# Token halves of the output projection swapped, the norm's gain moved into the FFN weights, and four rings re-used

## The chip, the cores and the metric

The kernel runs on one core of one Trainium2 chip. The metric is the device time of one execution in microseconds (us). Engine names: PE is TensorE's matmul, ACT is ScalarE, DVE is VectorE, POOL is GpSimd, SP is SyncE, which here issues every DMA transfer.

## What is computed

A trunk of two layers over 1024 tokens of width 1024, in float32. Layer 0 mixes by attention, layer 1 by a gated recurrence; each is followed by a gated feed-forward network (FFN) of inner width 2816. Every sub-layer has a norm ahead of it and one behind it.

```python
def rmsnorm(x, g):
    y = x * rsqrt(mean(x * x, axis=-1) + 1e-6)
    return y * g

for layer in range(2):
    h = rmsnorm(x, norm_mix_pre[layer])
    m = attention(h) @ attn_w_out  if layer == 0 else  recurrence(h) @ rg_w_out
    x = x + rmsnorm(m, norm_mix_post[layer])
    h = rmsnorm(x, norm_ffn_pre[layer])
    f = (silu(h @ w_gate) * (h @ w_up)) @ w_down
    x = x + rmsnorm(f, norm_ffn_post[layer])
```

## The kernel before

**Products.** Float32 accuracy comes from three fast matmuls: each operand is split into a rounded high part (an ACT cast) and the rest, the low part (a DVE subtraction), and PE adds high x high, high x low, low x high. A product of 128 x 512 outputs over a depth of 512 is 12 such matmuls. The FFN's products are cut by a Strassen-Winograd scheme: seven products where a plain block product has eight, at the price of sums of blocks (S1 to S4 on the weights' side, the tiles e and f on the tokens' side).

**Tokens** are handled in tiles of 128: tiles 0 to 3 are the first half, 4 to 7 the second.

**out_product** is the projection behind each mixer with both norms. It takes six tiles in two trios, first (0,1,4), then (2,3,5), each trio in six PSUM banks, and last the tiles 6 and 7 as plain float32 matmuls from unsplit weights, 16 matmuls each; those weight rows lie in the ring "w" (eight buffers of 4 KB per partition). For each tile it runs `post_norm` (L209) and `pre_norm` (L187): DVE multiplies the PSUM result by the gain into the tile mg (L215), ACT squares and sums (L168), POOL makes the inverse root rs (L170 to L172), DVE adds to x (L218), then ACT squares x, POOL makes the next rs, DVE makes h = x * rs * g (L195), PE transposes h in eight 128 x 128 pieces (L201), and `HiddenS.take` (ACT L75, DVE L78) builds the tokens' operands from the transposes: b0 from a first-half tile (its transposes are also kept, in f), b1 and b2 from a second-half tile together with the f of its partner. mg is also the buffer of h.

**gate_up** multiplies by the gate and up weights, 11 column groups each. `begin` makes ahead of time the two products of a column group that need b0 alone, for the first two groups of each. `blocks` loads a group's two weight tiles of 128 x 1024, makes the sums, casts each operand (`operand`, ACT L493, DVE L494) and runs the products, S2's first. With the two begun ones a block is seven products of 12 matmuls. **down** makes seven products into the rows of a result r = 0 or 1 of four tiles a each. It finishes row 1 first, runs the norms `norm(1, a)`, then the last products, and for each a the norm `norm(0, a)`. Row r, tile a is token tile 4*r + a: the second half comes first. Behind layer 0's `down` the hidden tiles go to **recurrent** instead, whose `xr` runs, for three column groups c, 24 matmuls over the first token half (L158 to L160) and then 24 over the second.

The order of the instructions on each engine is set by the scheduler when the kernel is built, from its own estimate of times. Each engine then runs its list strictly in order and waits on semaphores; SP does the same with the DMA list. A ring's buffer is free for its next tile when the last reader of the old one is through.

Of the kernel before, what the change touches and what calls it, by code (L numbers as in the profile page):

```python
# [45 lines left out]
class HiddenS:  # L46
# [5 lines left out]

    GROUPS = ((0, 2), (2, 1), (3, 4))

    def __init__(self, trunk, pool):
        self.nc, self.uid = trunk.nc, trunk.uid
        self.g = [[pool.tile([P, n, 4, 512], F32R, tag=f"b{i}{z}", name=trunk.uid("hS"))
                   for z in range(2)] for i, (_, n) in enumerate(self.GROUPS)]
        self.f = {}
# [6 lines left out]
    def take(self, t, ps, scratch, pool):  # L66
# [25 lines left out]
        f, e = self.f[t - 4], new("e", 1)  # L92
# [10 lines left out]
class Trunk:  # L103
# [4 lines left out]
    def __init__(self, ctx, tc, io):  # L108
# [15 lines left out]
        self.mark = None  # L124

# [61 lines left out]
    def pre_norm(self, pool, x, h, g, sink, t, psum):  # L187
# [9 lines left out]
        for q in range(2):  # L197
            ps = psum()
            for j in range(4):
                kt = 4 * q + j  # L200
                nc.tensor.transpose(ps[:, j * P:(j + 1) * P], h[:, kt * P:(kt + 1) * P], self.ident)  # L201
# [3 lines left out]
    def post_norm(self, ms, mg, x_src, x_dst, t, gpost, sink, pool, g=None):  # L205
# [14 lines left out]
        if sink is not None:  # L220
            self.pre_norm(pool, x, mg, g, sink, t, self.psum_t)
# [188 lines left out]
    def out_product(self, ap, aT, w, x_src, x_dst, gpost_v, g_v, sink, kts):  # L410
# [24 lines left out]
        def norm(t, ps):  # L435
            mg = ap.tile([P, D], F32, tag="mg", bufs=2, name=self.uid("mg"))
            ms = [(slice(i * 512, (i + 1) * 512), p) for i, p in enumerate(ps)]
            self.post_norm(ms, mg, x_src, x_dst, t, gpost, sink, ap, g)

        gpost = g = None  # L440
        bufs = {"act": 2, "ah": 3, "al": 3}
        for ts in ((0, 1, 4), (2, 3, 5)):
            pst = [[self.psum() for _ in range(2)] for _ in range(3)]
            for kt in kts:
                if g is None and kt == kts[0]:
# [13 lines left out]
            if g is None:  # L459
                gpost = self.gain(ap, "gpost", gpost_v)  # L460
                g = self.gain(self.apool, "first", g_v)
            for i in ((0, 1, 2) if ts[0] == 0 else (0, 2, 1)):
                norm(ts[i], pst[i])

        rows, acts = [], []
        for i, kt in enumerate(kts):
            raw = self.main.tile([P, 2, 512], F32, tag="w", bufs=8, name=self.uid("raw"))
            nc.sync.dma_start(raw, wv[kt])
            rows.append(raw)
            n = ("ah", "al", "act")[i % 3]  # L470
            acts.append(act(kt, (6, 7), ap.tile([P, 384], F32, tag=n, bufs=bufs[n], name=self.uid("act"))[:, :2 * P]))
        for t in range(2):
# [3 lines left out]
            norm(6 + t, ps)  # L476


    def gate_up(self, ap, hS, wg, wu, gO):
# [5 lines left out]
        nc, tt = self.nc, self.nc.vector.tensor_tensor  # L485
        n_op = [0]

        def operand(src):

            pool, tag, bufs = (self.main, "w", 8) if n_op[0] % 14 < 8 else (ap, "w2", 6)  # L490
            n_op[0] += 1
            t = pool.tile([P, 2, 4, P], F32R, tag=tag, bufs=bufs, name=self.uid("q"))
            self.last = nc.scalar.copy(t[:, 0], src).ins  # L493
            tt(t[:, 1], src, t[:, 0].bitcast(F32), op=ALU.subtract)  # L494
            return t

        def raw():
            return self.main.tile([P, 2, 4, P], F32, tag="raw", bufs=3, name=self.uid("raw"))

        def rows(w, k, c0, n):  # L500
            return w[k * 512:(k + 1) * 512, c0:c0 + n].rearrange("(k p) c -> p k c", p=P)
# [10 lines left out]
        def begin(w, j):  # L512

            r = raw()
            for k in range(2):
                nc.sync.dma_start(r[:, k], rows(w, k, j * 256, P))
            a11, a12 = operand(r[:, 0]), operand(r[:, 1])
            return product(a11, 0), product(a12, 1)

        def sums(p1, p2):  # L520
            c = [ap.tile([P, 512], F32, tag="c", bufs=11, name=self.uid("c")) for _ in range(4)]
            nc.scalar.copy(c[1], p1)  # L522
            tt(c[0], p2, c[1], op=ALU.add)
            return c

        def blocks(w, j, begun=None, after=None):


            a = []
            for k in range(2):  # L530
                r = raw().rearrange("p z k c -> p (z k c)").rearrange("p (k c) -> p k c", k=4)
                nc.sync.dma_start(r, rows(w, k, j * 256, 256))
                a.append(r)
            a11, a21 = a[0][:, :, 0:P], a[0][:, :, P:256]
            a12, a22 = a[1][:, :, 0:P], a[1][:, :, P:256]
            with self.tc.issue_after(after) if after else nullcontext():
                if begun is None:
                    begun = [product(operand(a11), 0), None]
                    begun[1] = product(operand(a12), 1)
                q = {}  # L540
                q["A22"] = operand(a22)
                tt(a22, a21, a22, op=ALU.add)
                tt(a21, a11, a21, op=ALU.subtract)
                tt(a11, a22, a11, op=ALU.subtract)
                q["S2"] = operand(a11)
                q["S3"] = operand(a21)
                q["S1"] = operand(a22)
                tt(a12, a12, a11, op=ALU.subtract)
                q["S4"] = operand(a12)
# [411 lines left out]
```

## Time and profile before

| | |
|---|---|
| median of 3 runs | 2275.26 us (2273.81 to 2275.34) |
| the profiled execution | 2271.51 us, span 2269.7 us |
| busy share of the span: PE, DVE, ACT, POOL | 97%, 70%, 44%, 7% |
| mean granted TensorE clock | 0.99 |
| stages: o0 (out_product, layer 0), then its FFN | about 514 to 617 us, 617 to 1285 us |
| recurrent; o2 (out_product, layer 1); its FFN | 1285 to 1510 us, 1514 to 1615 us, 1615 us to the end |

A row of the timeline gives the start, the length, the engine, the source line, the operation, what it writes and reads, its shape, and in brackets the idle time of the engine ahead of it with the instruction that ended it. Matmuls overlap: a 128 x 512 one is shown 0.39 us long, but the next starts 0.23 us behind it. A row of the groups gives busy us in all and mean ns of one, then the idle time ahead of them.

### The profile page before, as it was taken

Reading aid. Unit: us, or ns where it says so; the run is one execution under the profiler, and the core shown is the slowest. Engines: PE = TensorE matmul, PEld = TensorE weight load, DVE = VectorE, ACT = ScalarE, POOL = GpSimd, SP = SyncE. Lnnn points to the kernel's source line nnn. Section 1 sums busy time; section 2 is a strip of 40 time slices with the busy share of each in tenths; the row PEclk is TensorE's granted clock in tenths of the full one; section 3 lists DMA queues with packets and bytes.
Section 4 is the critical chain, followed back from the end, with each engine's and each line's share of the span. In section 5 each row is a group of like instructions: output and inputs, shape, how many; then the busy total and the mean of one; then the engine's idle time right before and its main releaser. Section 6 shows DMA issues by size and latency. Waiting matters only on the chain. (4 is left out here: it accounts for less than half of the span.)

```text
span 2269.7 us, 29965 instructions
## 1 busy us (share of the span) xinstructions
PE 2201.2 (97%) x10968; PEld 1794.1 (79%) x10968; DVE 1592.3 (70%) x2476; ACT 999.9 (44%) x1738; POOL 163.8 (7%) x370
## 2 busy tenths in 40 slices
PE   7999999999999999999999799999899999999998
PEld 6887888877678888888888577887578888888886
DVE  5676765464678777775867577626788777758676
ACT  4544455464543333332536567525533333324444
POOL 2111212131100000000001100001100000000010
PEclk9999999999999999999999899999999999999999
DMA  4101011125724333234558311257434333327456
GB/s 161 55 19 48 24 43 40 59 94 162 248 70 139 116 92 118 89 121 171 191 166 263 120 47 47 83 169 245 134 112 134 93 116 93 116 89 275 122 193 235
DMA packets 200100, 278.84 MB, mean 123 GB/s; under 512 B 14224, under 2 KB 127888, under 8 KB 199952
## 3 DMA queue, kind: packets, MB, share of 16 engines
q1 hardware_dynamic: 199952, 276.92, 38.0%
q8 instruction: 86, 1.41, 0.3%
q14 instruction: 62, 0.51, 0.1%
HBM read 211.33 MB, written 65.54 MB: 122 GB/s over the span
## 5 line engine op out<-in xcount | busy, mean ns | idle before, releaser
L507 PE MATMUL ps<-hS,q 128*128 128x512 f32 x1232 | 482.6, 392 | 13.4 <-ACT c L522 10.1
L508 PE MATMUL ps<-hS,q 128*128 128x512 f32 x1232 | 481.7, 391 | 1.5 <-DVE hS L78 1.5
L509 PE MATMUL ps<-hS,q 128*128 128x512 f32 x1232 | 481.0, 391 | 0.0
L493 ACT CAST q<-raw 128x512 fp32r<-128x512 f32 x308 | 187.0, 621 | 410.5 <-PE ps L509 154.4
L507 PEld LDWEIGHTS ps<-hS,q 128*128 128x128 f32 x1232 | 232.4, 189 | 65.0 <-ACT c L522 11.2
L508 PEld LDWEIGHTS ps<-hS,q 128*128 128x128 f32 x1232 | 232.7, 189 | 50.4 <-DVE hS L78 2.3
L509 PEld LDWEIGHTS ps<-hS,q 128*128 128x128 f32 x1232 | 232.5, 189 | 48.6
L494 DVE TENSOR_TENSOR q<-raw,q 128x512 fp32r<-128x512 f32 x308 | 209.1, 689 | 67.4 <-ACT q L493 64.4
L605 PE MATMUL ps<-o,o 128*128 128x512 f32 x616 | 239.8, 390 | 0.6 <-DVE o L600 0.6
L606 PE MATMUL ps<-o,o 128*128 128x512 f32 x616 | 237.6, 390 | 0.0
L604 PE MATMUL ps<-o,o 128*128 128x512 f32 x616 | 220.1, 391 | 3.2 <-ACT o L715 2.5
L599 ACT CAST o<-raw 128x512 fp32r<-128x512 f32 x206 | 123.8, 620 | 188.7 <-PE ps L606 57.7
L600 DVE TENSOR_TENSOR o<-raw,o 128x512 fp32r<-128x512 f32 x206 | 137.9, 688 | 58.1 <-ACT o L599 57.1
L148 DVE TENSOR_TENSOR wlo<-raw,whi 128x1024 fp32r<-128x1024 f32 x76 | 93.3, 1229 | 75.6 <-ACT whi L147 73.4
L604 PEld LDWEIGHTS ps<-o,o 128*128 128x128 f32 x616 | 115.4, 188 | 29.7 <-ACT o L715 4.4
L605 PEld LDWEIGHTS ps<-o,o 128*128 128x128 f32 x616 | 115.6, 188 | 25.0 <-DVE o L600 1.3
L606 PEld LDWEIGHTS ps<-o,o 128*128 128x128 f32 x616 | 115.6, 188 | 24.2 <-DVE o L716 0.4
L171 POOL TENSOR_SCALAR rs<-ss 128x1 f32<-128x1 f32 x64 | 25.7, 401 | 1267.4 <-ACT junk L168 1174.4
L147 ACT CAST whi<-raw 128x1024 fp32r<-128x1024 f32 x76 | 79.8, 1052 | 70.2 <-PE ps L159 24.7
L158 PE MATMUL psq<-hT,whi 128*128 128x512 f32 x256 | 101.2, 395 | 1.1 <-DVE v L255 1.1
L159 PE MATMUL psq<-hT,whi 128*128 128x512 f32 x256 | 100.9, 394 | 0.0
L160 PE MATMUL psq<-hT,wlo 128*128 128x512 f32 x256 | 100.5, 393 | 0.0
(184 smaller groups left out, 4103.4 us busy)
## 6 DMA issues: line engine op xcount, KB each, us to landing
raw<-in_ffn_w_down_dram SPq DMA_DIRECT2D x96, 256.0 KB, 4.3
raw<-in_ffn_w_gate_dram SPq DMA_DIRECT2D x44, 512.0 KB, 4.2
raw<-in_ffn_w_up_dram SPq DMA_DIRECT2D x44, 512.0 KB, 4.0
gS<-c SPq DMA_DIRECT2D x88, 256.0 KB, 2.2
raw<-gS SPq DMA_DIRECT2D x88, 256.0 KB, 2.8
gA<-c SPq DMA_DIRECT2D x66, 256.0 KB, 3.2
raw<-in_attn_w_in_dram SPq DMA_DIRECT2D x24, 512.0 KB, 4.0
raw<-in_attn_w_out_dram SPq DMA_DIRECT2D x24, 512.0 KB, 4.2
```

The source lines that it names most:

```text
L158: nc.tensor.matmul(ps, wh[:, kt, cols], hh[:, kt, :], start=kt == 0, stop=False)
L159: nc.tensor.matmul(ps, wh[:, kt, cols], hl[:, kt, :], start=False, stop=False)
L493: self.last = nc.scalar.copy(t[:, 0], src).ins
L494: tt(t[:, 1], src, t[:, 0].bitcast(F32), op=ALU.subtract)
L507: nc.tensor.matmul(ps, a[:, 0, kt, :], bh, start=kt == 0, stop=False)
L508: nc.tensor.matmul(ps, a[:, 0, kt, :], bl, start=False, stop=False)
L509: nc.tensor.matmul(ps, a[:, 1, kt, :], bh, start=False, stop=kt == 3)
L599: nc.scalar.copy(t[:, 0], src)
L600: tt(t[:, 1], src, t[:, 0].bitcast(F32), op=ALU.subtract)
L604: nc.tensor.matmul(ps, a[0], b[:, 0], start=first, stop=False)
L605: nc.tensor.matmul(ps, a[0], b[:, 1], start=False, stop=False)
L606: nc.tensor.matmul(ps, a[1], b[:, 0], start=False, stop=last)
```

## The change

The token halves change places: out_product takes the trios (4,5,0) and (6,7,1) and then the plain tiles 2 and 3; `HiddenS` builds b0 from tiles 4 to 7 and b1, b2 from tiles 0 to 3; `down` maps row r, tile a to tile 4*(1-r) + a, so that the first token half is normed first and the second last. `pre_norm` of the FFN no longer multiplies by the gain: ACT makes h = x * rs, and the 512 KB load of that gain goes. The gain is applied to the weights instead: in `begin` by four ACT and four DVE instructions of 128 x 128 for an operand that was one of each of 128 x 512, and in `blocks` by eight ACT instructions of 128 x 256, in place, ahead of the sums. The first mg of each trio, the f of tile 7 and the first two pairs of begun results take buffers of the ring "w"; the weight rows of the plain tiles are loaded ahead of the second trio's norms, two of the eight rows in the ring "raw" (three buffers), where the FFN's weights are loaded too. The second and third begun pairs are ordered behind the transposes of tiles 2 and 3. Silu is called within `blocks`. The diff, cut:

```diff
-        if t < 4:
-            f = self.f[t] = new("f", 2)
+        if t >= 4:
+            f = self.f[t - 4] = new("f", 2) if t != 7 else self.spare()
...
-        def norm(t, ps):
-            mg = ap.tile([P, D], F32, tag="mg", bufs=2, name=self.uid("mg"))
+        def norm(t, ps, own=True):
+            mg = (ap.tile([P, D], F32, tag="mg", bufs=2, name=self.uid("mg")) if own else
+                  self.main.tile([P, D], F32, tag="w", bufs=8, name=self.uid("mg")))
...
-        for ts in ((0, 1, 4), (2, 3, 5)):
+        for ts in ((4, 5, 0), (6, 7, 1)):
...
-            for i in ((0, 1, 2) if ts[0] == 0 else (0, 2, 1)):
-                norm(ts[i], pst[i])
-
-        rows, acts = [], []
-        for i, kt in enumerate(kts):
-            raw = self.main.tile([P, 2, 512], F32, tag="w", bufs=8, name=self.uid("raw"))
+            else:
+                rows, acts = [], []
+                for i, kt in enumerate(kts):
+                    tag, n = ("raw", 3) if i < 2 else ("w", 8)
+                    raw = self.main.tile([P, 2, 512], F32, tag=tag, bufs=n, name=self.uid("raw"))
...
+            for i in range(3):
+                norm(ts[i], pst[i], i > 0)
...
+                src, k0 = src
+                for k in range(4):
+                    g = gain[:, k0 + k:k0 + k + 1]
+                    nc.scalar.activation(t[:, 0, k], src[:, k], AF.Copy, scale=g)
+                    nc.vector.scalar_tensor_tensor(t[:, 1, k], src[:, k], g, t[:, 0, k].bitcast(F32),
+                                                   op0=ALU.mult, op1=ALU.subtract)
...
+            a = [operand((raw(w, k, j * 256, P, r[:, k]), 4 * k), False) for k in range(2)]
+            with self.tc.issue_after(after) if after else nullcontext():
+                return product(a[0], 0), product(a[1], 1)
...
+                    for i in range(4):
+                        nc.scalar.activation(a[k][:, i], a[k][:, i], AF.Copy, scale=gain[:, 4 * k + i:4 * k + i + 1])
...
-            begun[i] = begin(w, j)
+            begun.append(begin((wg, wu)[i % 2], i // 2, self.turned[i + 1] if i in (1, 2) else None))
             if i < 2:
-                begun[i] = sums(*begun[i])
+                o = self.main.tile([P, 2, 512], F32, tag="w", bufs=8, name=self.uid("first"))
+                nc.scalar.copy(o[:, 0], begun[i][0])
+                tt(o[:, 1], begun[i][1], o[:, 0], op=ALU.add)
+                begun[i] = o
...
-                    self.post_norm(ms, mg, x_src, x_dst, 4 * r + a, gpost, sink, ap)
+                    self.post_norm(ms, mg, x_src, x_dst, 4 * (1 - r) + a, gpost, sink, ap)
```

How the scheduled order moves is seen at two places. **PE, end of layer 0's `down`, before.** `pst<-ident` are the transposes of the last normed tiles, m1722 and m1723 being the hidden tiles a = 2 and 3 of row 0; `ps<-hT` is `xr` on the first token half (hT1925 its high part), on the second (hT1927).

```order
L606 MATMUL ps2066_11648<-o2014_11387,o2065_11645 128x512
L201 MATMUL pst2058_11619<-ident_63,m1722_9722 128x128 x4
L201 MATMUL pst2059_11624<-ident_63,m1722_9722 128x128 x4
L201 MATMUL pst2073_11700<-ident_63,m1723_9723 128x128 x4
L201 MATMUL pst2074_11705<-ident_63,m1723_9723 128x128 x4
L158 MATMUL ps2092_11760<-hT1925_10973,whi2076_11734 128x512
```

**The same place in the change**, where m1723 and m1724 are the tiles a = 2 and 3 (token tiles 6 and 7), hT1926 and hT1927 the high and low part of the first half, and hT1928 the high part of the second:

```order
L163 MATMUL ps2096_12018<-hT1926_11197,wlo2081_11966 128x512
L204 MATMUL pst2059_11843<-ident_63,m1723_9946 128x128 x4
L161 MATMUL ps2096_12018<-hT1926_11197,whi2080_11965 128x512
L162 MATMUL ps2096_12018<-hT1927_11198,whi2080_11965 128x512
L204 MATMUL pst2060_11848<-ident_63,m1723_9946 128x128 x4
L163 MATMUL ps2096_12018<-hT1926_11197,wlo2081_11966 128x512
...
L163 MATMUL ps2099_12052<-hT1926_11197,wlo2084_11973 128x512
L204 MATMUL pst2074_11924<-ident_63,m1724_9947 128x128 x4
L204 MATMUL pst2075_11929<-ident_63,m1724_9947 128x128 x4
L161 MATMUL ps2102_12086<-hT1928_11199,whi2077_11958 128x512
```

All 72 matmuls of `xr` on the first token half, 24 for each of ps2093, ps2096 and ps2099, now stand between the transposes of the last normed tiles and in part ahead of them; before, they stood behind the last transpose.

**ACT, start of layer 0's `gate_up`, before.** hS is written by `take` for the last tile, whose e and f are e1275 and f1233 (L75), c is a begun result, q1306 the operand A22 of the first block and q1307 that of its S2.

```order
L75 CAST hS1058_5604<-f1211_6273 128x2x4x128
L75 COPY e1275_6507<-pst1273_6497 128x512
L75 CAST hS1056_5602<-pst1274_6502 128x4x128
L75 CAST hS1058_5604<-e1275_6507 128x8x128
L75 CAST hS1058_5604<-f1233_6356 128x2x4x128
L522 COPY c1282_6626<-ps1279_6599 128x512
L493 CAST q1306_6746<-raw1305_6744 128x512
L522 COPY c1291_6667<-ps1288_6640 128x512
L570 ACT_TABLE_LOAD
L570 ACTIVATE c1281_6625<-c1281_6625 128x512
L493 CAST q1307_6752<-raw1304_6742 128x512
```

**The same place in the change**, where q1294 is a begun operand, the raw tiles are weights scaled in place by the gain, e1274 and f1237 belong to the last tile, q1299 is the operand A22 and q1300 that of S2:

```order
L77 CAST hS1058_5604<-e1261_6443 128x8x128
L508 ACTIVATE q1294_6747<-raw1292_6735,gcol_72 128x128 x2
L77 CAST hS1056_5602<-pst1273_6500 128x4x128
L77 CAST hS1058_5604<-f1226_6303 128x2x4x128
L543 ACTIVATE raw1298_6784<-raw1298_6784,gcol_72 128x256 x3
L77 COPY e1274_6505<-pst1272_6495 128x512
L543 ACTIVATE raw1298_6784<-raw1298_6784,gcol_72 128x256
L77 CAST hS1058_5604<-e1274_6505 128x8x128
L77 CAST hS1058_5604<-f1237_6342 128x2x4x128
L543 ACTIVATE raw1313_6892<-raw1313_6892,gcol_72 128x256 x4
L502 CAST q1299_6794<-raw1298_6784 128x512
L502 CAST q1300_6800<-raw1297_6782 128x512
```

The casts for the last tile and S2's operand now stand behind scaling instructions of two weight tiles and of begun operands, while the table load (L570 before) and the copies of begun results have left this place.

More of the change, by code (lines that the diff above doesn't have):

```diff
@@ L510, in product @@
             return ps
-        def begin(w, j):
-            r = raw()
-            for k in range(2):
[L516 to L533, printed above, removed]
+        def begin(w, j, after):
+            r = self.main.tile([P, 2, 4, P], F32, tag="raw", bufs=3, name=self.uid("raw"))
+            a = [operand((raw(w, k, j * 256, P, r[:, k]), 4 * k), False) for k in range(2)]
+            with self.tc.issue_after(after) if after else nullcontext():
+                return product(a[0], 0), product(a[1], 1)
@@ L534, in blocks @@
+        def blocks(w, j, begun, silu, after=None):
+            a = [raw(w, k, j * 256, 256) for k in range(2)]
+            for k in range(2):
+                with self.tc.issue_after(after) if after else nullcontext():
+                    for i in range(4):
+                        nc.scalar.activation(a[k][:, i], a[k][:, i], AF.Copy, scale=gain[:, 4 * k + i:4 * k + i + 1])
             a11, a21 = a[0][:, :, 0:P], a[0][:, :, P:256]
             a12, a22 = a[1][:, :, 0:P], a[1][:, :, P:256]
[L536 to L549, printed above, removed]
@@ L550, in blocks @@
-            c = sums(*begun) if len(begun) == 2 else begun
-            _, u2, u3, c22 = c
-            tt(u2, product(q["S2"], 4), u2, op=ALU.add)
+            q = {}
+            if begun is None:
+                q["A11"] = operand(a11)
+                q["A12"] = operand(a12)
+            q["A22"] = operand(a22)
+            tt(a22, a21, a22, op=ALU.add)
+            tt(a21, a11, a21, op=ALU.subtract)
+            tt(a11, a22, a11, op=ALU.subtract)
+            q["S2"] = operand(a11)
+            q["S3"] = operand(a21)
@@ new lines, in blocks @@
+            q["S1"] = operand(a22)
+            tt(a12, a12, a11, op=ALU.subtract)
+            q["S4"] = operand(a12)
+            c = [ap.tile([P, 512], F32, tag="c", bufs=11, name=self.uid("c")) for _ in range(4)]
+            c11, u2, u3, c22 = c
+            if begun is None:
+                begun = product(q["A11"], 0), product(q["A12"], 1)
+            if isinstance(begun, tuple):
+                nc.scalar.copy(u2, begun[0])
+                tt(c11, begun[1], u2, op=ALU.add)
+                p1, sum = u2, c11
+            else:
+                p1, sum = begun[:, 0], begun[:, 1]
@@ L553, in blocks @@
+            tt(u2, product(q["S2"], 4), p1, op=ALU.add)
             tt(u3, product(q["S3"], 5), u2, op=ALU.add)
@@ L913, in run @@
                                  io["rg_w_out"], xs[1], xs[2], io["norm_mix_post"][1],
[L914 removed]
+                                 hS, list(range(KT)))
             if stop == 2:
```

83 lines of the change are left out of this document (47 added, 36 removed).

## The prediction

> **What bounds the kernel now.** I read the page's busy shares first, then the table by stage, then PE's timeline where a stage is short of full.
>
> ```profile
> PE 2201.2 (97%) x10968; PEld 1794.1 (79%) x10968; DVE 1592.3 (70%) x2476; ACT 999.9 (44%) x1738; POOL 163.8 (7%) x370
> ```
>
> PE is busy 97% of the span: all its idle time is 2269.7 - 2201.2 = 68.5 us, and no change that leaves the products alone can win more than that and the time in which matmuls run slowly. Here the number of PE's instructions stays the same. The columns of the next table are the length, each engine's busy time (with its instructions), the granted clock, the DMA engines' share and GB/s.
>
> ```profile
> core 0: us, PE busy (x) PEld busy (x) DVE busy (x) ACT busy (x) POOL busy (x), PEclk, DMA share, GB/s
> 510.00:700.00 190.00, 179.66 (x765) 134.96 (x762) 129.77 (x177) 85.07 (x153) 15.10 (x40) 0.96 0.49 159
> 700.00:1200.00 500.00, 500.00 (x2206) 413.77 (x2205) 373.20 (x580) 177.02 (x300) 0.00 (x0) 1.00 0.42 135
> 1200.00:1300.00 100.00, 85.65 (x383) 68.31 (x382) 70.19 (x96) 61.53 (x103) 19.84 (x32) 0.91 0.61 195
> 1510.00:1700.00 190.00, 177.97 (x743) 135.22 (x743) 131.90 (x181) 87.92 (x156) 15.10 (x40) 0.98 0.54 176
> ```
>
> The long inner part of the FFN, 700 to 1200 us, has no PE idle time at all; a matmul there takes 500 / 2206 = 0.227 us. What can be won lies at the seams: 14.4 us idle at a clock of 0.91 in 1200 to 1300, where layer 0's `down` hands over to the recurrence, and 10 to 12 us each in 510 to 700 and 1510 to 1700, from out_product into `gate_up`. The change touches both kinds of seam, and puts work into the full part.
>
> **Seam one: `down` to the recurrence.** PE's timeline:
>
> ```profile
> 1261.62 1.10 PE L201 MATMUL pst<-ident,m 128*128 128x128 f32 x8 [0.32 <-ACT m L193]
> 1262.47 0.48 PE L606 MATMUL ps<-o,o 128*128 128x512 f32 x1
> ...
> 1268.75 1.09 PE L201 MATMUL pst<-ident,m 128*128 128x128 f32 x8 [0.32 <-ACT m L193]
> ...
> 1274.73 2.20 PE L201 MATMUL pst<-ident,m 128*128 128x128 f32 x8 [3.27 <-ACT m L193]
> 1285.36 1.97 PE L201 MATMUL pst<-ident,m 128*128 128x128 f32 x8 [8.43 <-ACT m L193]
> 1287.15 2.07 PE L158 MATMUL ps<-hT,whi 128*128 128x512 f32 x4
> 1289.02 0.63 PE L159 MATMUL ps<-hT,whi 128*128 128x512 f32 x1
> ...
> 1291.16 0.52 PE L158 MATMUL ps<-hT,whi 128*128 128x512 f32 x1
> ```
>
> Before, the first token half is normed last, so PE waits for its h (L193, in m) four times: 0.32 + 0.32 + 3.27 + 8.43 = 12.3 us. Then it is slow for a while: the eight transposes at 1285.36 hold PE 1.79 us instead of the 0.85 at 1261.62, and the nine matmuls from 1287.15 to 1291.16 take 4.0 us instead of 9 x 0.227 = 2.0; the transposes at 1274.73 are 1.1 us longer than those at 1261.62. Slowness costs 0.9 + 2.0 + 1.1 = 4.0, and the seam 16.3 us in all.
>
> After the swap the recurrence's first half needs no tile that is still being normed, and the order puts all its 72 matmuls, 16.3 us, between and ahead of the last transposes. Is that cover long enough for the last tile's chain? DVE's and ACT's parts of it:
>
> ```profile
> 1274.41 0.68 DVE L721 TENSOR_TENSOR m<-ps,m 128x512 f32<-128x512 f32 x1
> ...
> 1280.76 1.28 DVE L218 SCALAR_TENSOR_TENSOR x<-m,rs,x 128x1024 f32<-128x1024 f32 x1
> 1287.13 0.69 DVE L43 TENSOR_TENSOR hT<-pst,hT 128x512 fp32r<-128x512 f32 x1 [5.10 <-ACT hT L42]
> ```
>
> ```profile
> 1284.16 1.15 ACT L193 ACTIVATE m<-x,rs 128x1024 f32<-128x1024 f32 x1 [0.94 <-POOL rs L172]
> 1286.51 0.58 ACT L42 CAST hT<-pst 128x512 fp32r<-128x512 f32 x1 [1.21 <-PE pst L201]
> ...
> 1299.43 0.78 ACT L784 ACTIVATE xc<-ps,cols 128x512 f32<-128x512 f32 x1 [8.32 <-DVE carry L783]
> ...
> 1304.64 0.78 ACT L784 ACTIVATE xc<-ps,cols 128x512 f32<-128x512 f32 x1 [1.37 <-DVE carry L783]
> ...
> 1318.93 0.62 ACT L795 CAST xh<-xc 128x512 fp32r<-128x512 f32 x1 [0.74 <-DVE xc L793]
> ```
>
> From the sum of the last product (1274.41) over x (1280.76) and h (1284.16) to the transposes (1285.36) it takes 11.0 us. In the change 56 of the 72 matmuls stand behind the last matmul of `down`: 56 x 0.227 = 12.7 us, and 0.9 of other transposes. DVE came to the sum about 3 us after that last matmul (PE had run out at 1274.73 - 3.27 = 1271.46), since it had a queue; the 16 matmuls ahead (3.6 us) give it the time to work that off. The cover exceeds the chain by 2 to 3 us, so I take all the waits as gone, and the slow clock with them. What is late next: the second half's first matmul needs ACT's cast of the last transposes (0.58 us, 1286.51) and then DVE's subtraction (0.69, 1287.13), with nothing on PE to hide them now: 0.5 us lost. Behind it, `xr` hands its results through ACT and DVE to the gates' matmuls:
>
> ```profile
> 1321.93 0.39 PE L814 MATMUL ps<-xh,whi 128*128 128x512 f32 x1
> ```
>
> Before, the last operand that their start needs was cast at 1318.93 + 0.62 = 1319.55, so they had 2.4 us to spare. PE comes there 16 us earlier, but ACT and DVE can begin `xr`'s chain only when the last hidden tile is through, at about 1289 instead of 1299.43: 10.4 earlier. If that chain kept its 20.1 us, PE would wait 16.3 - 0.5 - 10.4 - 2.4 = 3.0. But before it was fed at PE's pace, one column group every 5.2 us (ACT's idle 1.37 ahead of 1304.64 ends with DVE's carry, which waits for PE); now three groups lie ready at once. I take 2.0 lost, with 1 and 4 as ends. Seam one: -16.3 + 0.5 + 2.0 = **-13.8 us**, ends -10 and -16.
>
> The Trainium skill, in TensorE: Matmul & The Clock Gate (section "What's actually happening"), says that the array falls to half clock after an idle window of about 3.4 us and returns after about 3.4 us of sustained work. By that the slowness behind the 8.43 us would cost 1.7 us instead of the 2.9 seen at 1285.36 to 1291.16, and my result would be 1.2 us later. The rows show the longer time, and they are what the sum uses.
>
> **Seam two: out_product into gate_up, twice.**
>
> ```profile
> 560.04 0.50 PE L432 MATMUL ps<-whi,ah 128*128 128x512 f32 x1 [3.27 <-ACT junk L168]
> ...
> 617.26 0.60 PE L201 MATMUL pst<-ident,mg 128*128 128x128 f32 x4
> 618.24 0.63 PE L201 MATMUL pst<-ident,mg 128*128 128x128 f32 x4 [0.37 <-DVE e L78]
> ...
> 620.05 0.96 PE L507 MATMUL ps<-hS,q 128*128 128x512 f32 x3 [0.93 <-ACT hS L75]
> 621.75 0.50 PE L508 MATMUL ps<-hS,q 128*128 128x512 f32 x1 [0.73 <-DVE hS L78]
> ...
> 645.54 0.80 PE L507 MATMUL ps<-hS,q 128*128 128x512 f32 x1 [4.64 <-ACT c L522]
> ...
> 653.07 0.39 PE L507 MATMUL ps<-hS,q 128*128 128x512 f32 x1
> ...
> 1642.18 0.79 PE L507 MATMUL ps<-hS,q 128*128 128x512 f32 x1 [5.26 <-ACT c L522]
> ```
>
> *Between the trios* PE waits 3.27 us until ACT has squared the third tile's result and its banks come free. The change gives that tile a buffer of its own, but ACT's list has the first tile's second square, which waits for x, ahead of the second tile's square; the bank comes about 0.5 us sooner, no more. I take -0.5, with -3.3 (all gone) and +1.5 (one more square and its reading) as ends.
>
> *The plain tiles.* The second trio's first mg lies in a buffer of "w" that held a weight's low part, and PE reads that up to the trio's last matmul. So the product with the gain starts only then, and the first plain tile's banks wait for it, where PE did not wait before.
>
> ```profile
> L215 DVE TENSOR_TENSOR mg<-ps,g 128x512 f32<-128x512 f32 x32 | 20.8, 684 | 8.6 <-PE pst L201 6.0 <-PE ps L432 2.6
> ```
>
> Two of them at 0.6 us apart and a semaphore: +1.4; ends 0 (ACT's squares, also needed, are later anyway) and 2.5.
>
> *To the first S2 product.* Count from the last plain matmul, which ends where the transposes at 617.26 start. Before, PE waits 0.37 + 0.93 + 0.73 for the first half's operand, does begun products, waits 4.64 for a copied result to free its bank, runs 24 matmuls, the first nine of them slowly, and starts S2 at 653.07: 35.8 us. In layer 1 the copy's wait is 5.26. In the change the three small waits go: the first half has long been normed. But the last two tiles now feed b1 and b2, which only S2 and its fellows read, while the weights come late: two rows of plain weights sit in "raw" until nearly the last plain matmul, so the begun operands 3 and 4 are loaded and made behind it, in time in which before they lay ready.
>
> ```profile
> raw<-in_ffn_w_gate_dram SPq DMA_DIRECT2D x44, 512.0 KB, 4.2
> ```
>
> ```profile
> L493 ACT CAST q<-raw 128x512 fp32r<-128x512 f32 x308 | 187.0, 621 | 410.5 <-PE ps L509 154.4 <-DVE raw L544 131.6 <-issue 51.3
> L335 ACT ACTIVATE pr<-pr,mn 128x128 f32<-128x128 f32 x8 | 3.2, 400 | 0.8 <-DVE mn L327 0.7
> L331 ACT ACTIVATE pr<-sc 128x128 f32<-128x128 f32 x8 | 2.2, 282 | 2.2 <-PE tr L356 2.2
> L335 ACT ACTIVATE pr<-pr,mn 128x256 f32<-128x256 f32 x8 | 4.0, 505 | 2.5 <-DVE mn L327 2.5
> L360 ACT COPY pt<-tr 128x256 f32<-128x256 f32 x36 | 13.3, 372 | 14.3 <-PE tr L356 14.1
> L75 ACT CAST hS<-e 128x1024 fp32r<-128x1024 f32 x8 | 8.4, 1050 | 12.3 <-DVE e L78 12.3
> ```
>
> After that matmul a load takes 4.2 us. An operand of `begin` was one cast, 0.52 us apart; four scalings of 128 x 128 cost 4 x 0.3 = 1.2 (0.28 without a scale and 0.40 with a bias from a column, less the 0.1 that neighbours overlap). A weight tile in place costs 4 x 0.41 = 1.6 (0.37 to 0.51, the same way). Following ACT's list by these durations, the last tile's transposes come about 17 us behind the last plain matmul, and from there ACT has ahead of S2's cast: four begun operands 4.8, two weight tiles 3.3, five casts for b1 and b2 of about 1 us and two of 0.5 with a copy 5.6, and A22's cast 0.5: 14.2 us. Three sums on DVE (1.8), a cast and a subtraction (1.2) follow: S2 at 35.2 to 35.9, PE idle before it about 6.4. That is where it was; only now the slow clock after the long idle falls behind S2 and is not in it, 2.0 us as at 645.54 (nine matmuls in 4.0). I take **+2.0**, with -3 (the small waits gone and ACT ready in time) and +5 (one more load in the chain) as ends.
>
> Per layer -0.5 + 1.4 + 2.0 = +2.9, twice +5.8.
>
> **The full part, and the rest.** In a block ACT gains 8 x 0.41 = 3.3 us and DVE nothing. A block is 84 matmuls, 19.1 us; ACT is busy 177 of 500 us, so 35% + 17% = 52% of it after the change. Loading, scaling, sums and the first cast take about 4.2 + 3.3 + 2 + 1 = 10.5 us of a buffer's turn, under 19.1. I cost it at nothing; the cover is the remaining 8.6 us. The gain's load goes, and DVE's sixteen products with it pass to ACT's scaled copies (1.15 as at 1284.16 for 1.28): nothing on PE's path, which waits for others there.
>
> ```profile
> L195 DVE SCALAR_TENSOR_TENSOR mg<-x,rs,g 128x1024 f32<-128x1024 f32 x16 | 20.5, 1283 | 17.2 <-POOL rs L172 17.2
> ```
>
> The table load and the order of silu: nothing, as PE is not waiting for them.
>
> **Sum.** -13.8 + 5.8 = -8.0 us, against the profiled execution 2271.51 - 8.0 = 2263.5. The median of the runs stands 3.75 us above the profiled execution (2275.26), which I carry over: **2267.3 us**.
>
> **Rivals.**
> 1. *Seam two loses its waits too.* For it: the order now has b0 done early, and all of layer 0's waits at that seam (3.27 + 0.37 + 0.93 + 0.73 + 4.64 = 9.9) have one of the changed buffers at their end. Against it: ACT's list of 14.2 us. If half goes in both layers, -13.8 - 9.9 = -23.7: 2251.6 us. Chance 0.24.
> 2. *The gain of seam one is given back.* The recurrence's gates wait for ACT and DVE by the full 4 us, again in the next column groups (its stage has ACT and DVE chains of the same kind), and half remains: -7 + 5.8 = -1.2: 2274 us. For it: 2.4 us to spare and no more. Against: groups ready at once. Chance 0.20.
> 3. *Slower: scaling lengthens the blocks.* If a weight buffer's turn is longer than I add up (silu and copies of products sit in the same ACT list, and a cast may stand behind the next block's scaling), PE waits in each of about 40 blocks. It decides from (8.0 + 4.6) / 40 = 0.3 us a block; at 0.6 us the sum is -8.0 + 24 = +16: 2291 us. Against: PE has no idle time there now and 8.6 us of cover. Chance 0.09.
> 4. *The swap does nothing*, since the scheduler's order is one thing and the waits another: if the last tile's norm is held by `xr`'s ACT work, seam one keeps its waits and +5.8 remains: 2281 us. Against: in ACT's list the casts of the last tile stand ahead of `xr`'s. Chance 0.04.
>
> **How the numbers follow.** My forecast has 0.43, with its own range 2260 to 2275 from the ends of its terms. What lies below 2252 needs rival 1 in more than half; what lies above 2279 needs 3 or 4. So the range is 2252 to 2279. A difference under 0.2%, 4.6 us, can't be told from none. Faster than that is below 2270.7: of the forecast 0.37, rival 1 with 0.24, of rival 2 0.06: 0.67. Within: 0.06 of the forecast, 0.14 of rival 2 and 0.02 of 3: 0.22. Slower: 0.11.
>
> **What would show it.** In the profile of the changed kernel: 1200 to 1300 with under 3 us of PE idle time and a clock near 1; the last transposes of that seam without a wait; the gates' first matmuls waiting 1 to 4 us for xh. Between the trios a wait of 2 to 3 us, about 1.4 ahead of the first plain tile, and one of about 6 ahead of S2 that ends with a cast or subtraction of q. ACT at about 50% in 700 to 1200, PE at no idle time there. I am wrong if seam one still waits for h, if PE shows idle time in the blocks, or if S2 starts far from 35 us behind the plain tiles.

## The result

The changed kernel takes 2288.36 us (median of 4 runs, 2286.91 to 2293.99); the kernel before took 2274.53 us beside it. The ratio is 1.0066, with a 95% interval of 1.0048 to 1.0084: slower by 13.8 us where 8 us of gain had been forecast. (The ratio, here and below, is to the kernel before, run beside the other.) The profiled execution took 2288.38 us, its span is 2286.6 us: 16.9 us more than before. The 3.75 us by which the median stood above the profiled execution before, and which the forecast carried over, are not there now.

PE's own rows split that into stages. The times below run from one of PE's events to the next: from out_product's first matmul, over the last one of its plain tiles, the first matmul of S2 and the first one of `down`, to the next out_product.

| stage, us | before | changed | difference | forecast |
|---|---|---|---|---|
| layer 0: both trios and the plain tiles | 102.6 | 103.5 | +0.9 | +0.9 |
| layer 0: plain tiles' end to S2 | 35.6 | 37.3 | +1.6 | 0 |
| layer 0: S2 to `down` (22 blocks) | 398.5 | 410.4 | **+11.9** | +2.0 |
| `down` and the recurrence | 462.1 | 447.2 | **-14.9** | -13.8 |
| layer 1: trios and plain tiles | 101.4 | 104.4 | +2.9 | +0.9 |
| layer 1: plain tiles' end to S2 | 34.6 | 38.2 | +3.6 | 0 |
| layer 1: S2 to `down` | 398.9 | 409.6 | **+10.7** | +2.0 |

(The start and the last `down` make up the rest, +1.4 and -1.2. The forecast's +2.0 us a layer at the second seam are slow matmuls behind the first S2 product, so they stand in the row of the blocks.) The forecast's gain came. Of its losses, the slow matmuls came as priced: 2.1 us in either layer. S2 itself was 1.6 and 3.6 us late, and layer 1's trios and plain tiles cost 2 us more than forecast. What turned the sign is the rest of the blocks' loss, about 18 us, which the forecast had costed at nothing. Measured as time beyond 0.227 us a matmul, layer 0 lost 6.2 us between 667 and 712 us, where the same place lost 1.4 before, and 4.8 us from 950 us on, where nothing was lost before. In layer 1 it was 6.3 for 1.8, and 4.0.

The page's busy shares, and the table by stage for the FFN's inner part and for the first seam (which now lies 16 us later):

```profile
PE 2208.8 (97%) x10968; PEld 1791.5 (78%) x10968; DVE 1560.0 (68%) x2508; ACT 1149.1 (50%) x2154; POOL 165.3 (7%) x370
```

```profile
core 0: us, PE busy (x) PEld busy (x) DVE busy (x) ACT busy (x) POOL busy (x), PEclk, DMA share, GB/s
700.00:1200.00 500.00, 494.65 (x2165) 406.38 (x2164) 366.43 (x585) 223.87 (x439) 0.00 (x0) 1.00 0.40 128
1216.00:1316.00 100.00, 97.52 (x456) 79.39 (x455) 79.23 (x111) 67.49 (x111) 23.17 (x32) 1.00 0.62 198
```

In 700 to 1200 us, where PE had no idle time before, it is now idle for 5.35 us and passes 2165 matmuls instead of 2206: 41 matmuls, 9.3 us of work, did not get through. ACT is at 45% there, 224 us for 177, so it is not short of time. The first seam has 2.5 us idle at full clock, where 14.4 at 0.91 were. PE's rows there:

```profile
1288.95 1.03 PE L204 MATMUL pst<-ident,m 128*128 128x128 f32 x8
...
1303.93 1.04 PE L204 MATMUL pst<-ident,m 128*128 128x128 f32 x8
1305.21 0.97 PE L161 MATMUL ps<-hT,whi 128*128 128x512 f32 x3 [0.24 <-ACT hT L42]
...
1323.97 0.73 PE L840 MATMUL ps<-xh,whi 128*128 128x512 f32 x2 [0.74 <-ACT xh L821]
```

The transposes have no wait left. The second half's first matmul waits 0.24 us (0.5 had been taken), the gates' first one 0.74 (2.0). PE's rows at the second seam and in the blocks:

```profile
555.96 0.50 PE L436 MATMUL ps<-whi,ah 128*128 128x512 f32 x1 [0.55 <-ACT junk L171]
...
590.20 4.99 PE L436 MATMUL ps<-raw,act 128*128 128x512 f32 x11 [2.48 <-ACT junk L171]
...
629.50 0.63 PE L204 MATMUL pst<-ident,mg 128*128 128x128 f32 x4 [2.95 <-DVE e L80]
...
656.94 0.79 PE L524 MATMUL ps<-hS,q 128*128 128x512 f32 x1 [7.09 <-ACT q L502]
...
704.24 0.50 PE L524 MATMUL ps<-hS,q 128*128 128x512 f32 x1 [1.87 <-ACT q L502]
...
974.36 0.50 PE L524 MATMUL ps<-hS,q 128*128 128x512 f32 x1 [1.19 <-DVE c L570]
...
1014.96 0.50 PE L524 MATMUL ps<-hS,q 128*128 128x512 f32 x1 [1.15 <-DVE c L570]
```

Between the trios PE waits 0.55 us for the third tile's square where it waited 3.27, but two new waits of 0.34 and 0.93 us for VectorE stand ahead of it: 1.82 us in all, where 2.8 had been forecast. The wait ahead of the plain tiles is 2.48, where 1.4 had been. S2 starts behind a wait of 7.09 us, 37.3 us after the plain tiles (35.2 to 35.9 had been worked out, and a wait of 6.4). The last three rows are new: long waits inside the blocks, at the start of the fourth, and then near the end of the stage, with some 265 us between them in which PE runs at full pace. In layer 0 before, the blocks' waits were 0.23 and 0.18 us, in the first two blocks alone.

### The profile page after: what moved, and what is told of

The parts are those of the page before. It is cut to its first block, busy times and chain, and to the rows that moved or that the text cites. A ratio compares the mean times of both kernels' runs of the same rounds, so it can differ in the third digit from the quotient of the medians.

```text
span 2286.6 us, 30327 instructions
## 1 busy us (share of the span) xinstructions
PE 2208.8 (97%) x10968; PEld 1791.5 (78%) x10968; DVE 1560.0 (68%) x2508; ACT 1149.1 (50%) x2154; POOL 165.3 (7%) x370
## 4 chain that ended last, share of the span: by engine, by line
PE 52%; DVE 17%; DMA 14%; ACT 10%; issue 6%; POOL 1%; SPq 0%; ACTq 0%; POOLq 0%; DVEq 0%
DMA raw<-in_ffn_w_up_dram 5%; PE ps L436 5%; DVE q L503 4%; DMA raw<-in_ffn_w_gate_dram 4%; ACT raw L543 4%; PE ps L630 3%; PE ps L631 3%; PE ps L632 3%; PE pso L369 3%; PE tr L360 3%; PE ps L524 3%; PE ps L525 3%; PE ps L526 3%; PE psq L162 3%; PE psq L161 3%
## 5 line engine op out<-in xcount | busy, mean ns | idle before, releaser
L503 DVE TENSOR_TENSOR q<-raw,q 128x512 fp32r<-128x512 f32 x292 | 195.9, 688 | 170.1 <-ACT q L502 169.5
L543 ACT ACTIVATE raw<-raw,gcol 128x256 f32<-128x256 f32 x352 | 150.8, 498 | 226.4 <-DMA raw<-in_ffn_w_up_dram 112.1
L502 ACT CAST q<-raw 128x512 fp32r<-128x512 f32 x292 | 166.6, 615 | 127.7 <-DVE raw L553 123.8
L364 ACT COPY pt<-tr 128x512 f32<-128x512 f32 (+1 forms) x128 | 65.5, 527 | 77.9 <-PE tr L360 77.4
L161 PE MATMUL psq<-hT,whi 128*128 128x512 f32 x256 | 101.2, 395 | 1.1 <-DVE v L259 1.1
```

Of the source, the lines that this page charges most:

```text
L161: nc.tensor.matmul(ps, wh[:, kt, cols], hh[:, kt, :], start=kt == 0, stop=False)
L543: nc.scalar.activation(a[k][:, i], a[k][:, i], AF.Copy, scale=gain[:, 4 * k + i:4 * k + i + 1])
```

## Experiments

The kernel before took 2273.12 us beside the first four of these runs and 2271.43 us beside the last three, for 2274.53 beside the changed kernel, so differences to the changed kernel are uncertain by two or three microseconds.

Two theories stood after the result. **Theory A**: the scaling of the blocks' weights is what costs, because of where it stands in ScalarE's list. **Theory B**: the cost comes from the rest of the change, the swap in out_product, the rings, or from ScalarE's added work as such. How the loop of theory A runs is seen in the changed kernel's trace. ACT:

```profile
941.46 1.71 ACT L543 ACTIVATE raw<-raw,gcol 128x256 f32<-128x256 f32 x4 [2.71 <-DMA raw<-in_ffn_w_up_dram]
943.08 0.60 ACT L502 CAST q<-raw 128x512 fp32r<-128x512 f32 x1
...
948.23 1.71 ACT L543 ACTIVATE raw<-raw,gcol 128x256 f32<-128x256 f32 x4 [2.51 <-DMA raw<-in_ffn_w_gate_dram]
949.84 0.60 ACT L502 CAST q<-raw 128x512 fp32r<-128x512 f32 x1
953.91 1.66 ACT L502 CAST q<-raw 128x512 fp32r<-128x512 f32 x3 [3.47 <-DVE raw L553]
961.35 1.71 ACT L543 ACTIVATE raw<-raw,gcol 128x256 f32<-128x256 f32 x4 [5.78 <-DMA raw<-in_ffn_w_gate_dram]
```

DVE (L503 is an operand's low part, L551 the first of the block's sums):

```profile
943.71 0.69 DVE L503 TENSOR_TENSOR q<-raw,q 128x512 fp32r<-128x512 f32 x1 [4.33 <-ACT q L502]
...
951.21 0.69 DVE L551 TENSOR_TENSOR raw<-raw,raw 128x512 f32<-128x512 f32 x1
...
956.38 0.69 DVE L503 TENSOR_TENSOR q<-raw,q 128x512 fp32r<-128x512 f32 x1
```

SP, the loads of the weight tiles:

```profile
916.64 0.37 SPq L517 DMA_DIRECT2D raw<-in_ffn_w_gate_dram  x1
...
937.51 0.38 SPq L517 DMA_DIRECT2D raw<-in_ffn_w_up_dram  x1
...
944.43 0.38 SPq L517 DMA_DIRECT2D raw<-in_ffn_w_gate_dram  x1
...
957.09 0.37 SPq L517 DMA_DIRECT2D raw<-in_ffn_w_gate_dram  x1
...
997.73 0.37 SPq L517 DMA_DIRECT2D raw<-in_ffn_w_gate_dram  x1
```

A load issued at 937.51 lands, and ACT scales its tile from 941.46 (an idle time ahead that ends with the DMA). Behind it in ACT's list stands the S4 cast of the block ahead (943.08), whose low part (943.71) is the last reader of another buffer of "raw". Only then is the next load issued: 944.43. That load's tile is scaled from 948.23, and behind that stands a cast of the current block (949.84) on which its sums (951.21) wait; they release S2's and S3's casts (953.91), S3's low part (956.38) frees a buffer, and the next load goes at 957.09. So one turn holds both loads of a block and both tiles' scalings one after the other. Over two blocks, 916.64 to 957.09 and 957.09 to 997.73, it takes 40.4 and 40.6 us: 20.3 us a block, where PE needs 19.1. From the rows, about 8.2 us of the 20.3 are loads (issue to scaling), 3.2 scalings and 8.9 casts, subtractions and sums. The operands made ahead cover the difference until the wait at 974.36; from there on PE is held at the loop's pace (974.36 to 1014.96 is 40.6 us). In the kernel before, the same loads go at PE's pace, 38.1 us apart for two blocks:

```profile
895.95 0.37 SPq L532 DMA_DIRECT2D raw<-in_ffn_w_gate_dram  x1
...
934.03 0.37 SPq L532 DMA_DIRECT2D raw<-in_ffn_w_gate_dram  x1
```

The early wait falls in the first four blocks. Their two products from b0 were begun ahead, so PE has only five products there, 60 matmuls or 13.6 us, and a turn has to be shorter still. The load issued at 690.13 us gives the operand of the S2 product at 704.24, 14.1 us later, with ScalarE's scaling (694.06), casts and VectorE's sums on the way.

**The row mapping alone.** In the kernel before:

```diff
-                    self.post_norm(ms, mg, x_src, x_dst, 4 * r + a, gpost, sink, ap)
+                    self.post_norm(ms, mg, x_src, x_dst, 4 * (1 - r) + a, gpost, sink, ap)
```

With this line alone the product's rows and the token tiles no longer belong together; the instructions are the same.

> The kernel before with one line of the change alone: down maps row r, tile a to token tile 4*(1-r)+a, so that the recurrence's first half is normed first. Everything else, out_product's trios and the gain in the norm, is as before. My theory (the change's gain is all at that seam, 14.9 us between the traces): PE loses its waits of 3.27 and 8.43 us there and the slow clock, about -14 us: 2260 us, 1200 to 1300 us with under 3 us idle. Rival (the gain there came only together with the rest of the change, or is given back in the recurrence): 2270 us or more.

Measured: 2253.21 us against 2273.12, ratio 0.9916 (0.9901 to 0.9930). Down and recurrence take 445.6 us for 462.1, -16.5.

```profile
1200.00:1300.00 100.00, 98.06 (x459) 79.92 (x458) 79.83 (x112) 67.52 (x111) 23.62 (x32) 1.00 0.62 195
```

PE is busy 98.06 of 100 us at clock 1.00. The gain needs nothing but the mapping. It is somewhat larger than expected, since gate_up, with the same instructions, also came out 2.0 to 2.5 us shorter in each layer. In layer 0 the order on every engine is the same there; most of the difference is matmuls that ran 0.43 us apart before, from 622.66 to 625.64 us behind the waits of 0.93 and 0.73, and that run at full pace here behind the same two waits. In layer 1 the order differs a little as well. Why PE slows in one run and not in the other is not settled.

**The blocks without scaling.** In the changed kernel:

```diff
-            for k in range(2):
-                with self.tc.issue_after(after) if after else nullcontext():
-                    for i in range(4):
-                        nc.scalar.activation(a[k][:, i], a[k][:, i], AF.Copy, scale=gain[:, 4 * k + i:4 * k + i + 1])
```

> The changed kernel without the eight scalings of each block's two weight tiles. It leaves out the norm's gain for all weights but the begun operands', so this is a measurement of what the scaling costs and no version. My theory (the scaling makes the loading loop of a block 20.3 us long where PE needs 19.1, and stands before S2): the waits behind S2 in both gate_up stages, 11.8 us in layer 0, fall to 2 us, and S2 starts 3 us earlier: 2288 - 24 = 2264 us. Rival (the loss in the blocks comes from the new rings, the results in the weights' ring or silu's new place, not from the scaling): within 4 us of the changed kernel, 2284 to 2288.

Measured: 2264.17 us, ratio 0.9965 (0.9953 to 0.9978). The stretches from the plain tiles to S2, and from S2 to `down`:

```profile
618.10:652.00 33.90, 26.30 (x121) 21.32 (x119) 31.69 (x64) 25.06 (x55) 3.22 (x7) 0.91 0.28 94
652.00:1051.40 399.40, 399.40 (x1753) 330.28 (x1754) 304.70 (x471) 130.79 (x218) 0.00 (x0) 0.99 0.33 108
```

33.9 and 399.4 us, where the changed kernel has 37.3 and 410.4; no idle time is left in the blocks. The expectation holds in both parts: without the blocks' scaling 14.3 us of gate_up go in layer 0 and 12.8 in layer 1. With rings, swap and silu's place kept, the long waits in the blocks are gone, so the rival's causes, rings and silu's place, don't make them by themselves. Only the slow matmuls right behind S2 stay (2.1 us).

**The same scaling, placed later.** The changed kernel, with each block's scalings ordered behind the S4 cast of the block ahead:

```diff
-                with self.tc.issue_after(after) if after else nullcontext():
+                with self.tc.issue_after(after or self.s4) if after or self.s4 else nullcontext():
...
             q["S4"] = operand(a12)
+            self.s4 = n_op[1]
...
-                nc.scalar.copy(t[:, 0], src)
+                n_op[1] = nc.scalar.copy(t[:, 0], src).ins
```

> The changed kernel with the same instructions, but the scalings of a block are ordered behind the S4 cast of the block ahead on ScalarE. My theory (it is not ScalarE's 3.4 us of work for a block but its place: a scaling that waits for its load holds the S4 cast behind it, which frees the buffer of the next load, so two loads and two scalings of 5.6 us stand in one loop): the loop falls to about 14 us, the waits near the end of gate_up (4.1 us idle and slow matmuls in layer 0) vanish, 2288 - 2 x 5 = 2278 us, with the early waits at 704 us perhaps as they are. Rival (ScalarE's added work is the cost wherever it stands): within 3 us of the changed kernel.

Measured: 2269.38 us, ratio 0.9987 (0.9978 to 0.9997).

```profile
620.20:656.80 36.60, 26.67 (x120) 21.21 (x118) 31.97 (x63) 29.74 (x67) 3.23 (x7) 0.93 0.25 87
656.80:1056.80 400.00, 399.78 (x1753) 330.62 (x1754) 302.59 (x472) 193.58 (x382) 0.00 (x0) 0.99 0.33 108
```

S2 starts as late as in the changed kernel (36.6 us), but the blocks take 400.0 us instead of 410.4, with ACT just as busy (193.6 us for 189.2). ACT, and the loads of every second block's second tile:

```profile
942.75 0.62 ACT L503 CAST q<-raw 128x512 fp32r<-128x512 f32 x1 [2.10 <-PE ps L527]
943.27 3.31 ACT L544 ACTIVATE raw<-raw,gcol 128x256 f32<-128x256 f32 x8
...
961.79 0.62 ACT L503 CAST q<-raw 128x512 fp32r<-128x512 f32 x1 [1.36 <-PE ps L527]
962.31 3.31 ACT L544 ACTIVATE raw<-raw,gcol 128x256 f32<-128x256 f32 x8
```

```profile
939.22 0.37 SPq L518 DMA_DIRECT2D raw<-in_ffn_w_gate_dram  x1
...
977.30 0.37 SPq L518 DMA_DIRECT2D raw<-in_ffn_w_gate_dram  x1
```

The eight scalings now stand behind the S4 cast (942.75, 961.79) and wait for no load; casts wait for PE or DVE. The loads are 38.1 us apart for two blocks, 19.0 a block: PE's own pace. Ten microseconds a layer were the place and not the work. The gain is 18 to 19 us and not the 10 expected, as the early waits at 704 us went too, with the slow matmuls behind them.

**The gain back in the norm.** The changed kernel, with h = x * rs * g on VectorE again and no scaling of weights:

```diff
-            self.pre_norm(pool, x, mg, None, sink, t, self.psum_t)
+            self.pre_norm(pool, x, mg, g, sink, t, self.psum_t)
...
-                    for i in range(4):
-                        nc.scalar.activation(a[k][:, i], a[k][:, i], AF.Copy, scale=gain[:, 4 * k + i:4 * k + i + 1])
...
-            a = [operand((raw(w, k, j * 256, P, r[:, k]), 4 * k), False) for k in range(2)]
+            a = [operand(raw(w, k, j * 256, P, r[:, k])) for k in range(2)]
```

> The changed kernel with the gain put back into the norm, on VectorE as before the change, and no scaling of weights in begin or in the blocks. Swapped halves, rings and places of the transposes stay. My theory (scaling is what costs): seam one keeps its 14 to 15 us, the blocks' waits go (-10 us a layer), S2 starts earlier by the 4.8 and 3.3 us of scaling on ScalarE (-3 to -6 us a layer): 2288 - 28 = 2260 us, or less. Rival (the swap in out_product and the rings cost at the second seam): seam two stays 3 us or more behind the kernel before in each layer, 2270 us or more.

Measured: 2256.39 us, ratio 0.9934 (0.9920 to 0.9949).

```profile
619.50:653.40 33.90, 27.75 (x122) 21.96 (x122) 31.97 (x43) 20.06 (x36) 4.85 (x10) 0.90 0.29 94
653.40:1050.70 397.30, 397.29 (x1753) 328.79 (x1752) 303.97 (x471) 130.35 (x218) 0.00 (x0) 1.00 0.34 108
```

S2 at 33.9 us and 397.3 us of blocks: the whole of gate_up is 431.2 us, 16.4 shorter than in the changed kernel and 2.9 shorter than before. Out_product, with its new rings and loads, is 1.0 us longer than before in layer 0 and 2.4 in layer 1, and gate_up is 2.1 shorter there. So the rest of the change, swap, rings and transposes' places, costs nothing in gate_up; over both stages it gains 2.0 us in layer 0 and loses 0.3 in layer 1.

**Begin without scaling.** The changed kernel with one cast and one subtraction for begin's operands:

```diff
-            a = [operand((raw(w, k, j * 256, P, r[:, k]), 4 * k), False) for k in range(2)]
+            a = [operand(raw(w, k, j * 256, P, r[:, k])) for k in range(2)]
```

> The changed kernel without the scaling of begin's operands: one cast and one subtraction of 128x512 each as before, so the gain is left out for the begun products and this is a measurement of its cost alone. The blocks' scaling stays. Theory (the blocks' scaling is the cost, begin's is a small part of the way to S2): S2 starts 1 to 3 us earlier than 37.3 us behind the plain tiles, the 410 us from S2 to down stay: 2288 - 4 = 2284 us. Rival (the 16 small scalings ahead of S2 carry the late start, and with it the early waits): S2 at 33 us or before, 2275 us or less.

Measured: 2268.68 us, ratio 0.9987 (0.9978 to 0.9996): not 2284.

```profile
618.20:651.50 33.30, 26.81 (x122) 21.19 (x119) 28.71 (x41) 24.69 (x45) 4.58 (x7) 0.95 0.29 95
651.50:1058.10 406.60, 401.66 (x1753) 328.98 (x1754) 295.42 (x471) 188.21 (x382) 0.00 (x0) 1.00 0.32 106
```

S2 comes at 33.3 us, 4.0 earlier, and the blocks take 406.6, 3.8 less; the wait ahead of S2 in layer 0 is 3.35 us. The rival's number is the better one here: the sixteen small scalings have a larger part than theory A gave them. With an earlier S2 no matmuls run 0.43 us apart behind the early waits, and the waits of 1.19 and 1.15 us near the end become 0.57 and 0.68. The blocks still carry 8 us more than before in layer 0 and 4.6 in layer 1. The parts don't add up: leaving out begin's scaling gains 17 to 20 us, the blocks' 23 to 24, but both together, with the gain on VectorE (the run before this one), 31 to 32.

**The swap alone.** The kernel before, with trios, plain tiles, `take` and mapping swapped:

```diff
-        if t < 4:
-            f = self.f[t] = new("f", 2)
+        if t >= 4:
+            f = self.f[t - 4] = new("f", 2)
...
-        for ts in ((0, 1, 4), (2, 3, 5)):
+        for ts in ((4, 5, 0), (6, 7, 1)):
...
-            acts.append(act(kt, (6, 7),
+            acts.append(act(kt, (2, 3),
...
-            norm(6 + t, ps)
+            norm(2 + t, ps)
...
-                    self.post_norm(ms, mg, x_src, x_dst, 4 * r + a, gpost, sink, ap)
+                    self.post_norm(ms, mg, x_src, x_dst, 4 * (1 - r) + a, gpost, sink, ap)
```

> The kernel before with the token halves swapped throughout and nothing else: trios (4,5,0) and (6,7,1), plain tiles 2 and 3, b0 from tiles 4 to 7, down's rows mapped to 4*(1-r)+a; gain in the norm, rings and loads as before. Theory (seam one is all of the gain, seam two is only relabelled by the swap): out_product and gate_up as long as before within 3 us, the seam to the recurrence 15 to 17 us shorter: 2254 to 2259 us, as the kernel with the mapping alone, and the best version. Rival (a gain at the first seam needs the other half of the change too, or the swap lengthens out_product): 2265 us or more.

Measured: 2255.11 us, ratio 0.9923 (0.9911 to 0.9936), from five rounds. That is 30 to 33 us below the changed kernel and 16 to 19 below the one before, and the fastest version of the whole computation here, though its interval meets that of the version with the gain in the norm. At the first seam PE waits only here:

```profile
1285.96 0.97 PE L158 MATMUL ps<-hT,whi 128*128 128x512 f32 x3 [0.24 <-ACT hT L42]
...
1304.72 0.73 PE L814 MATMUL ps<-xh,whi 128*128 128x512 f32 x2 [0.74 <-ACT xh L795]
```

Its layer 0 takes 73.2 us for the trios (73.3 before) and 431.7 for gate_up: the swap only relabels the second seam and gains at the first. In layer 1 the trios are 2.9 us longer, with the same wait of 3.3 us between them; the difference is thirteen matmuls that run 0.43 us apart behind it (1541.47 to 1546.59 us), where before none did.

**A fourth buffer.** The changed kernel, every fourth raw weight tile in a buffer of its own, and one operand buffer less:

```diff
-                into = self.main.tile([P, 4, n], F32, tag="raw", bufs=3, name=self.uid("raw"))
+                n_raw[0] += 1
+                into = (ap.tile([P, 4, n], F32, tag="raw4", bufs=1, name=self.uid("raw")) if n_raw[0] % 4 == 0 else
+                        self.main.tile([P, 4, n], F32, tag="raw", bufs=3, name=self.uid("raw")))
...
-        rings = [("w", 8)] * 8 + [("w2", 6)] * 6
+        rings = [("w", 8)] * 8 + [("w2", 5)] * 5
```

> The changed kernel with a fourth buffer for the blocks' raw weight tiles, and for its space one operand buffer less (5 in w2, 13 in the cycle). The scaling stays, ScalarE's order is left to the scheduler. Theory (the loop of 20.3 us a block runs through the free buffer of the next load): with four, a block's two loads no longer wait for the block just ahead, the loop opens, and the 410 us from S2 to down fall to about 400 as with the scalings placed late: 2288 - 2 x 9 = 2270 us. Rival (the cost is ScalarE's order, in which a scaling waits for its load ahead of casts, whatever the buffers): 405 to 412 us, 2280 us or more.

Measured: 2271.53 us, ratio 1.0000 (0.9990 to 1.0010).

```profile
622.00:659.90 37.90, 26.58 (x120) 21.16 (x118) 32.44 (x64) 31.86 (x72) 3.56 (x7) 0.91 0.30 98
659.90:1061.40 401.50, 399.45 (x1752) 330.01 (x1753) 296.56 (x471) 191.81 (x377) 0.00 (x0) 1.00 0.32 106
```

S2 stays late (37.9 us), and the blocks take 401.5 us: the forecast of this run and not its rival. The waits near the end are gone, part of the early ones stays (1.56 us at 677.77). So the ring of three buffers belongs to the loop as well as the place of the scalings. But the scheduler gave ScalarE another order in this run, with a block's two loads issued together (930.52) and scaled nearly together (935.01 and 937.14), so the buffer and the order that came with it are not told apart.

## Why the prediction was wrong

*Seam one* was right in its mechanism and nearly in its size: 14.9 us gained for 13.8. All waits for h went, and the slow clock with them. The 0.5 and 2.0 us charged for the second half's casts and the gates are 0.24 and 0.74 in the trace. With the mapping alone the seam gave 16.5 us, where the rows before had shown 16.3 to be lost.

*Between the trios and the plain tiles* the sum of both terms was right in layer 0 (+0.9 us, forecast -0.5 + 1.4), but by luck: the waits between the trios fell by 1.45 and the one ahead of the plain tiles is 2.48, so both terms were off by a microsecond, in opposite directions. In layer 1 it was +2.9; there PE waits another 1.37 us for an ACT cast in the trio, of which the forecast knew nothing.

*To the first S2 product* the chain through ACT's list came out nearly: 37.3 us for 35.2 to 35.9, and a wait of 7.09 for 6.4. (The terms that the prediction names, 17 + 14.2 + 1.8 + 1.2, add up to 34.2; it doesn't say what the other 1.0 to 1.7 are.) So S2 was 1.6 us later than before where it had been forecast at its old place, and 3.6 in layer 1. The slow matmuls behind it cost 2.1 us for 2.0. Without begin's scaling S2 comes 4.0 us earlier.

*The full part* is the step that failed. It said that loading, scaling, sums and the first cast take 10.5 us of a buffer's turn, under a block's 19.1, and costed the scaling at nothing. The scaling was sized rightly: 3.3 us for both tiles of a block, 3.2 in the trace. What the 10.5 us left out is the rest of the turn. They hold one load of 4.2 us, where the order as scheduled has a block's two loads in series, 8.2; and 3 us of sums and casts, where the turn has 8.9. The loads are in series since ScalarE takes its list in order: a scaling that waits for its load keeps back the cast behind it, and the low part of this cast's operand is the last reader of the buffer that the next load needs. The turn is 20.3 us, so there were 1.2 us too much in place of 8.6 us of cover. By these figures a turn without the scalings would be about 17 us, an estimate, under the 19.1; the runs without them show no loss there. Besides, the first four blocks of a layer have five products and not seven, 13.6 us and not 19.1, which the prediction did not count; there the early waits stand. Together the blocks lost 9.7 and 8.6 us beyond what stood there before and the priced slow matmuls, not evenly but at the two ends of the stage.

This is rival 3 in its mechanism (a cast may stand behind the next block's scaling), which had a chance of 0.09. It decides from 0.3 us a block and was priced at 0.6; the mean over the 44 blocks is 0.4. "PE has no idle time there now and 8.6 us of cover" was the argument against it, and the second half of that was the error. Idle time in the blocks was one of its own signs of being wrong, and 5.35 us of it came in 700 to 1200 us. The order of the change was at hand, and following the loads of one block through ACT's list, as was done for the way to S2, would have shown two loads in one turn. ACT's share of work, 45% where 52% had been worked out, told nothing of it.

*Rival 1* (the second seam loses its waits too) has no support: 7.09 and 2.48 us stand there. *Rivals 2 and 4* are refuted by the gates' 0.74 us and the transposes without a wait.

## What to carry to other kernels

Work moved to a lightly used engine costs what its place in that engine's list costs: an instruction that waits for a transfer keeps back whatever stands behind it, and if that frees the buffer of the next transfer, transfers run one after the other. So a moved step is to be followed through one whole turn of the ring, counting every load and every cast in it, and not by the engine's share; and a stage's shortest blocks, not its usual ones, say how long a turn may be. And where the next stage reads one half first, that half should be finished first: the mapping of one line was worth 15 to 17 us.

## What was not expected of the hardware

The durations of the new instructions were close to their estimates:

```profile
L543 ACT ACTIVATE raw<-raw,gcol 128x256 f32<-128x256 f32 x352 | 150.8, 498 | 226.4 <-DMA raw<-in_ffn_w_up_dram 112.1 <-DMA raw<-in_ffn_w_gate_dram 69.8 <-DVE c L603 29.2
L508 ACT ACTIVATE q<-raw,gcol 128x128 fp32r<-128x128 f32 x64 | 19.8, 395 | 0.0
```

A scaling of 128 x 128 takes 0.395 us alone, four of 128 x 256 take 1.71 us, 0.40 apart (0.41 had been taken).

The clock was less regular than its use in the forecast. In the changed kernel a wait of 1.87 us, at 704.24, is followed by slow matmuls, but only 1.4 us later:

```profile
705.62 0.63 PE L525 MATMUL ps<-hS,q 128*128 128x512 f32 x1
706.05 0.63 PE L524 MATMUL ps<-hS,q 128*128 128x512 f32 x1
```

From 705.62 to 708.61 they are 0.43 us apart. Before, the waits of 3.27 us between the trios, one in each layer, came out differently. In layer 0 matmuls run 0.43 us apart from 561.16 to 564.14; in layer 1 none does:

```profile
561.16 0.63 PE L432 MATMUL ps<-wlo,ah 128*128 128x512 f32 x1
561.58 0.63 PE L432 MATMUL ps<-whi,al 128*128 128x512 f32 x1
```

```profile
1559.33 0.50 PE L432 MATMUL ps<-whi,ah 128*128 128x512 f32 x1 [3.27 <-ACT junk L168]
1559.67 0.40 PE L432 MATMUL ps<-wlo,ah 128*128 128x512 f32 x1
1559.91 0.39 PE L432 MATMUL ps<-whi,al 128*128 128x512 f32 x1
```

With the swap alone, a wait of 3.29 us at layer 1's place was followed by thirteen. So the length of a single wait does not tell whether matmuls slow down behind it, nor for how long: the same wait cost nothing or nearly 3 us. The Trainium skill, TensorE: Matmul & The Clock Gate (section "What's actually happening"), has a window of about 3.4 us that runs freely. That the shorter wait slows PE and the longer one may not agrees with a window that isn't bound to the wait. The same section of the Trainium skill has the clock fall "after ≥1 idle window (~3.4µs)"; the wait of 1.87 us is shorter than that and was followed by slow matmuls all the same.
